# Last column block of a SwiGLU output product: token half 2 of its last four steps taken behind half 1, LayerNorm and output per half

## The chip, the cores and the metric

The kernel runs on one core of one Trainium2 chip. The core has a matrix engine (TensorE, "PE" in the profile, its weight loads "PEld"), a vector engine (VectorE, DVE), a scalar engine (ScalarE, ACT), GpSimd (POOL) and SyncE (SP), which issues most of the DMAs. The engines run at the same time, each takes its own instructions in order, and they wait for each other by semaphores. PE writes only to the small accumulator memory PSUM; the other engines read it from there. The metric is the device time of one execution in microseconds (us), the median of several runs.

## The reference

One decoder layer at batch 1, 256 tokens, width 2048, in float32. The change lies in the last lines, the second product of the SwiGLU (5632 to 2048) and the LayerNorm behind it:

```python
h = x * (1.0 + sc2) + sh2
gate, up = jnp.split(h @ w_ffn_in, 2, axis=-1)
y = (jax.nn.silu(gate) * up) @ w_ffn_out          # (256, 5632) @ (5632, 2048)
r = DEEPNORM_ALPHA * x + g2 * y
mu, var = r.mean(-1), jnp.square(r - r.mean(-1)).mean(-1)
x = (r - mu) * lax.rsqrt(var + LN_EPS) * ln2_g + ln2_b
```

The mean and the variance run over all 2048 columns of a token, so no token can be normalized before its last column is done.

## The kernel before

The 256 tokens are two halves of 128 (h = 0 and 1; "half 1" and "half 2" in the prediction), one token for each partition. A weight comes in tiles of 128x1024 that SP loads (`load_w`, L212, six buffers). ACT casts each to the reduced type float32r (`hi`, L221, four buffers), and DVE takes the rest (`lo`, L222, four buffers); PE multiplies with both, and so gets nearly full float32 precision. The activations are split the same way (`ach`, `acl`).

The output product is cut into four column blocks of 512 (`n` = 0 to 3). One block is 22 steps of two 128-row pieces of the weight each (`xs_unit`). A step has twelve products of 128x128 with 128x512: for each piece and each half, xh by hi (L356), xh by lo (L357) and xl by hi (L358). They add up in two PSUM tiles, `box[0]` and `box[1]`. Within a step the halves alternate; in the last step of a block half 1 comes ahead of half 2. `run(3)` writes the program so that about three splits are issued ahead of the step that PE is at. A scheduler then orders each engine's instructions by dependences and priorities.

At the end of a block `resid` (L1090) makes for each half t = ps*g2 (L1096), r = ALPHA*r + t (L1097) and bn_stats (L1098), and `fin` (L1315) multiplies r by the LayerNorm's gain (L1320). Behind the last block, `stats` (L1102) aggregates the mean and variance of both halves (L1106) and finds 1/sqrt(var + eps) with a Newton step (`rsqrt`, L365 to L372, its square root on ACT). `finish` (L1326) forms from -mean*rs, split in two, and ones a tile z of five columns; PE turns it (L1334) and ACT copies it to `zt` (L1336). With `rows`, five rows made of the gain and the bias, the product zt*rows (L1346, five rows deep) is the part of the output that isn't r*rs. DVE puts both together for every block of 128x512, r*rs + zt*rows (L1347), eight times, and SP writes the result out (L1351 for three blocks of both halves, 512 KB each, L1349 for the last block, 256 KB for each half).

The instructions in the names: `rt` is t, `st` the statistics, `mv` mean and variance, `le`, `lr`, `lrs` the steps of 1/sqrt, `mm` a PSUM tile of the pool with four such tiles, `tpm` the PSUM tile of the turned z, `raw` a loaded weight tile.

Of the kernel before, what the change touches and what calls it, by code (L numbers as in the profile page):

```python
# [93 lines left out]
def layer(ctx, tc, a, out):  # L94
# [995 lines left out]
    def resid(ps, c0, cn, gb, base, dst, st, n, then):  # L1090
        cc = slice(c0, c0 + cn)
        last = c0 + cn == D
        with tc.high_priority(offset=400 if last else 0):
            for h in range(2):
                t = acc("rt", [P, 512])[:, :cn]
                v_.tensor_tensor(t, ps[h], gb[:, cc], op=OP.mult)  # L1096
                v_.scalar_tensor_tensor(dst[:, h, cc], base[:, h, :], ALPHA, t, op0=OP.mult, op1=OP.add)  # L1097
                v_.bn_stats(st[:, h, n, :], dst[:, h, cc])  # L1098
# [190 lines left out]
    def fo_begin():  # L1289
        drain("main")  # L1290
        drain("ada")
        b0 = perm.tile([P, 2, D], F32, tag="s0", name="b0")
# [16 lines left out]
        cur["st"] = perm.tile([P, 2, 4, 6], F32, tag="stt", name="st2", bufs=2)

    do(fo_begin)
    for n, (c0, cn) in enumerate((512 * n, 512) for n in range(4)):
# [2 lines left out]
        def fin(ps, n=n, c0=c0, cn=cn):  # L1315
            cc = slice(c0, c0 + cn)
            r = cur["r"]
            resid(ps, c0, cn, cur["g2b"], r[:, :, cc], r, cur["st"], n, finish)
# [7 lines left out]
    def finish(mv, rs):  # L1326
        nm = perm.tile([P, 2, 1], F32, name="nm")
        z = cur["z"]
        v_.scalar_tensor_tensor(nm, mv[:, :, 0:1], -1.0, rs, op0=OP.mult, op1=OP.mult)
        v_.tensor_copy(z[:, :, 0:3:2], nm.to_broadcast([P, 2, 2]))  # L1330
        v_.tensor_tensor(z[:, :, 4:5], nm, z[:, :, 0:1].bitcast(F32), op=OP.subtract)
        tp = pt.tile([P, 512], F32, tag="tp", name="tpm")
        for h in range(2):
            t_.transpose(tp[0:5, h * P:(h + 1) * P], z[:, h, :].bitcast(F32), ident)  # L1334
        zt = cur["zt"] = cur["k3"].tile([5, 2, P], F32R, name="zt")
        s_.copy(zt, tp[0:5, :S].rearrange("p (h i) -> p h i", h=2))  # L1336
        cur["rs"] = rs
# [4 lines left out]
    for n in range(4):
        cc = slice(512 * n, 512 * n + 512)
        for h in range(2):
            ps = mm()
            t_.matmul(ps, cur["zt"][:, h], cur["rows"][:, cc], start=True, stop=True)  # L1346
            v_.scalar_tensor_tensor(r[:, h, cc], r[:, h, cc], rs[:, h], ps, op0=OP.mult, op1=OP.add)  # L1347
            if n == 3:
                dma.dma_start(out[0, h * P:(h + 1) * P, cc], r[:, h, cc])  # L1349
        if n < 3:  # L1350
            dma.dma_start(out[0, :, cc].rearrange("(h p) n -> p h n", p=P), r[:, :, cc])  # L1351
# [34 lines left out]
```

## Time and profile before

| | |
|---|---|
| time, median of 3 runs | 1697.94 us (1695.81 to 1700.74) |
| the profiled execution | 1696.81 us |
| its span, first to last instruction | 1694.9 us |
| mean granted clock of PE over the span | 0.994 of full speed |
| loads of the output product's weight | 88 of 512 KB, 4.1 us from issue to landing |
| ACT in the last column's steady state | a cast of 1.06 us every 2.72 us |

A row of the timeline has the start in us, the duration, the engine, the line of the kernel, the operation and its operands, shapes and count; in brackets the time that the engine was idle before it and what it waited for. A group's row has the operands, the count, the busy time in us and the mean of one in ns. Durations of PE overlap, since products are pipelined: the distance between starts says what one costs.

### The profile page before, as it was taken

To read this page: it belongs to the slowest core of one execution; us is meant where nothing else is said; L and a number is where in the kernel's file an instruction comes from. 1 tells how busy PE (TensorE), PEld (TensorE's weight loads), DVE (VectorE), ACT (ScalarE), POOL (GpSimd) and SP (SyncE) were. 2 spreads that over 40 slices of the span, in tenths; PEclk is the share of its full clock that TensorE was granted. 3 is DMA by queue.
4 is the path that set the end of the run, shared out by engine and by line. 5 is a ranking of instruction groups with operands and counts; after the bars stand their busy time and mean duration, and the time that the engine had idled before them with its cause. 6 is when DMAs were issued, how large, how long until landed. Compare 5 with 4: busy or idle time off the path is not lost.

```text
span 1694.9 us, 28166 instructions
## 1 busy us (share of the span) xinstructions
PE 1646.1 (97%) x11077; PEld 1478.7 (87%) x11077; DVE 1236.2 (73%) x1768; ACT 839.8 (50%) x1199; POOL 34.6 (2%) x60
## 2 busy tenths in 40 slices
PE   5899999999999999999999999999999999999997
PEld 4899999789989789889988898888888888888885
DVE  6899999687985678468998786666666666555454
ACT  3544445679653754464434454444444444333341
POOL 0000000001010000000000000000000000000000
PEclk9999999999999999999999999999999999999998
DMA  9999996566875578657999477777777777766651
GB/s 370 339 362 342 362 347 217 182 189 202 265 246 173 177 230 278 200 174 266 334 366 338 139 236 234 240 230 228 222 237 231 228 227 246 238 192 191 198 191 73
DMA packets 113751, 412.72 MB, mean 244 GB/s; under 512 B 13406, under 2 KB 14446, under 8 KB 108110
## 3 DMA queue, kind: packets, MB, share of 16 engines
q1 hardware_dynamic: 110178, 400.13, 70.2%
q0 software_dynamic: 3440, 10.80, 2.4%
q8 instruction: 87, 1.43, 0.3%
q14 instruction: 46, 0.37, 0.1%
HBM read 406.59 MB, written 4.28 MB: 242 GB/s over the span
## 4 chain that ended last, share of the span: by engine, by line
PE 62%; DVE 7%; DMA 4%; ACT 3%; issue 2%; POOL 0%; DVEq 0%; ACTq 0%; POOLq 0%
PE mm L315 17%; PE mm L319 9%; PE mm L356 7%; PE mm L358 7%; PE mm L357 7%; PE mm L308 4%; PE mm L309 4%; PE mm L310 3%; DVE lo L222 3%; DMA raw<-in_w_out 1%; DVE raw_a L241 1%; ACT hi L221 1%; DMA raw<-in_w_proj_gdn 1%; PE ps L756 1%; DMA UU<-ubd 0%
## 5 line engine op out<-in xcount | busy, mean ns | idle before, releaser
L222 DVE TENSOR_TENSOR lo<-raw,hi 128x1024 fp32r<-128x1024 f32 (+2 forms) x576 | 675.5, 1178 | 365.4 <-ACT hi L221 362.6
L221 ACT CAST hi<-raw 128x1024 fp32r<-128x1024 f32 (+2 forms) x576 | 583.6, 1017 | 721.5 <-PE mm L315 196.1
L308 PE MATMUL mm<-s,hi 128*128 128x256 f32 x1232 | 349.0, 284 | 16.1 <-ACT s L229 12.0
L310 PE MATMUL mm<-s,lo 128*128 128x256 f32 x1232 | 345.2, 281 | 8.1 <-DVE lo L222 7.9
L309 PE MATMUL mm<-s,hi 128*128 128x256 f32 x1232 | 345.1, 280 | 0.0
L315 PE MATMUL mm<-s,hi 128*128 128x512 f32 x1280 | 319.6, 392 | 0.0
L315 PEld LDWEIGHTS mm<-s,hi 128*128 128x128 f32 x1280 | 228.5, 188 | 39.5
L308 PEld LDWEIGHTS mm<-s,hi 128*128 128x128 f32 x1232 | 234.1, 190 | 21.3 <-ACT s L229 13.6
L310 PEld LDWEIGHTS mm<-s,lo 128*128 128x128 f32 x1232 | 234.1, 190 | 10.0 <-DVE lo L222 9.9
L309 PEld LDWEIGHTS mm<-s,hi 128*128 128x128 f32 x1232 | 234.4, 190 | 1.8 <-issue 1.4
L319 PEld LDWEIGHTS mm<-s,lo 128*128 128x128 f32 x1280 | 169.9, 188 | 13.6
L319 PE MATMUL mm<-s,lo 128*128 128x256 f32 x1280 | 171.9, 277 | 0.0
L357 PE MATMUL mm<-lo,ach 128*128 128x512 f32 x352 | 137.0, 389 | 0.0
L356 PE MATMUL mm<-hi,ach 128*128 128x512 f32 x352 | 137.0, 389 | 0.0
L358 PE MATMUL mm<-hi,acl 128*128 128x512 f32 x352 | 136.9, 389 | 0.0
L241 DVE CUSTOM_DVE_ANT_0 r<-r,cb,cols 128x2048 f32<-128x2048 f32 x40 | 93.5, 2348 | 9.2 <-ACT cb L137 9.2
L356 PE MATMUL mm<-hi,s 128*128 128x512 f32 x192 | 78.2, 407 | 0.0
L358 PEld LDWEIGHTS mm<-hi,acl 128*128 128x128 f32 x352 | 66.1, 188 | 13.8
L356 PEld LDWEIGHTS mm<-hi,ach 128*128 128x128 f32 x352 | 66.1, 188 | 13.7
L357 PEld LDWEIGHTS mm<-lo,ach 128*128 128x128 f32 x352 | 66.1, 188 | 13.5
L358 PE MATMUL mm<-hi,s 128*128 128x512 f32 x192 | 77.0, 401 | 0.0
L357 PE MATMUL mm<-lo,s 128*128 128x512 f32 x192 | 76.1, 396 | 0.0
(314 smaller groups left out, 2260.2 us busy)
## 6 DMA issues: line engine op xcount, KB each, us to landing
raw<-in_w_ffn_in SPq DMA_DIRECT2D x176, 512.0 KB, 4.3
raw<-in_w_in SPq DMA_DIRECT2D x160, 512.0 KB, 4.6
raw_a<-in_w_ada SPq DMA_DIRECT2D x112, 512.0 KB, 4.6
raw<-in_w_ffn_out SPq DMA_DIRECT2D x88, 512.0 KB, 4.1
r<-in_w_ada SPq DMA_DIRECT2D x40, 1024.0 KB, 8.1
raw<-in_w_in SPq DMA_DIRECT2D x48, 384.0 KB, 5.6
raw<-in_w_proj_gdn SPq DMA_DIRECT2D x32, 512.0 KB, 4.6
raw<-in_w_out SPq DMA_DIRECT2D x32, 512.0 KB, 6.3
```

Of the source, the lines that this page charges most:

```text
L221: s_.copy(hi, raw)
L222: low = v_.tensor_tensor(lo, raw, hi.bitcast(F32), op=OP.subtract)
L241: added = v_.tensor_tensor_reduce(out=raw, in0=raw, in1=cb[:, n * part:n * part + n], scale=1.0, scalar=cols[:, col:col + 1] if first else ...
L308: t_.matmul(o, hi[:, i, c], ah, start=(first and i == 0 and t == 0), stop=False)
L309: t_.matmul(o, hi[:, i, c], al, start=False, stop=False)
L310: t_.matmul(o, lo[:, i, c], ah, start=False, stop=(last and i == kn - 1 and t == 1))
L315: t_.matmul(box[t].rearrange("p (u i) -> p u i", u=2), hi[:, i, t * P:(t + 1) * P], both[k0 + i], start=(first and i == 0), stop=False)
L319: t_.matmul(box[t][:, :S], lo[:, i, t * P:(t + 1) * P], both[k0 + i][:, 0, :], start=False, stop=(last and i == kn - 1))
L356: t_.matmul(box[h], xh, hi[:, i, :], start=start, stop=False)
L357: t_.matmul(box[h], xh, lo[:, i, :], start=False, stop=False)
L358: t_.matmul(box[h], xl, hi[:, i, :], start=False, stop=stop)
L756: t_.matmul(ps[to, n, :], lhs(n), rhs(n), start=True, stop=True)
```

## The change

The last stage is written anew as `fo_unit`, `fo_column`, `scaled`, `fo_stats`, `fo_turn` and `fo_out`.

- In the blocks n = 0 to 2 the products stay in their order. Behind them come for both halves t, r and bn_stats, and then the scaling, at normal priority.
- In the block n = 3 the first 18 steps are as before. In the last four (`HOLD = 4`) only half 1's products are made at their place; the weights are kept, and half 2's products of the four steps follow in one piece.
- `end` puts half 1's statistics and scaling, which need only `box[0]`, ahead of half 2's held products, and half 1's turn of z and output behind them. Each half has its own z, zt and statistics. The square root is taken from the variance directly, with eps as its bias.
- Half 1's output is made by PE and ACT: PE multiplies a diagonal matrix of rs (`dg`, made by ACT from the identity) with r in plain float32, adds zt*rows in the same PSUM tile, and ACT copies the sum to r. Half 2's output is made by DVE as before. Two of half 1's PSUM tiles (`ps_o`) come from another pool.
- There are eight writes of 256 KB, one for each half and block.

```diff
+    def fo_column(ps, h, cc, n):
+        r = cur["r"]
+        t = acc("rt", [P, 512])
+        v_.tensor_tensor(t, ps, cur["g2b"][:, cc], op=OP.mult)
+        v_.scalar_tensor_tensor(r[:, h, cc], r[:, h, cc], ALPHA, t, op0=OP.mult, op1=OP.add)
+        v_.bn_stats(cur["st"][:, h, n, :], r[:, h, cc])
+
+    def scaled(h, cc):
+        r = cur["r"]
+        v_.tensor_tensor(r[:, h, cc], r[:, h, cc], cur["g"][:, cc], op=OP.mult)
+
+    def fo_stats(h):
+        own = cur["k3"].tile([P, 8], F32, name=f"fo{h}")
+        mv, e, q, rs, nm = [own[:, c:d] for c, d in ((0, 2), (2, 3), (3, 4), (4, 5), (5, 6))]
+        z = cur["z"][h]
+        v_.bn_aggr(mv, cur["st"][:, h])
+        s_.activation(q, mv[:, 1:2], AF.Sqrt, bias=epsc[:, 1:2])
+        v_.tensor_scalar(e, mv[:, 1:2], epsc[:, 1:2], -0.5, op0=OP.add, op1=OP.mult)
+        v_.reciprocal(q, q)
+        v_.tensor_tensor(rs, q, q, op=OP.mult)
+        v_.tensor_tensor(rs, rs, e, op=OP.mult)
+        v_.scalar_tensor_tensor(rs, rs, 1.5, q, op0=OP.add, op1=OP.mult)
+        v_.scalar_tensor_tensor(nm, mv[:, 0:1], -1.0, rs, op0=OP.mult, op1=OP.mult)
+        v_.tensor_copy(z[:, 0:3:2], nm.to_broadcast([P, 2]))
+        v_.tensor_tensor(z[:, 4:5], nm, z[:, 0:1].bitcast(F32), op=OP.subtract)
+        return rs
+
+    def fo_turn(h, rs):
+        tp = pt.tile([P, 512], F32, tag="tp", name="tpm")
+        t_.transpose(tp[0:5, :P], cur["z"][h].bitcast(F32), ident)
+        zt = cur["k3"].tile([5, P], F32R, name=f"zt{h}")
+        s_.copy(zt, tp[0:5, :P])
+        dg = k3_tile("sg")[:, 0, :P]
+        s_.activation(dg, ident, AF.Copy, scale=rs)
+        return zt, dg
+
+    def fo_out(h, n, rs, zt, dg, by_pe):
...
+        if by_pe:
+            t_.matmul(ps, dg, r[:, h, cc], start=True, stop=False)
+        t_.matmul(ps, zt, cur["rows"][:, cc], start=not by_pe, stop=True)
+        if by_pe:
+            s_.copy(r[:, h, cc], ps)
+        else:
+            v_.scalar_tensor_tensor(r[:, h, cc], r[:, h, cc], rs, ps, op0=OP.mult, op1=OP.add)
+        dma.dma_start(out[0, h * P:(h + 1) * P, cc], r[:, h, cc])
+
+    HOLD = 4
...
+        def end():
+            fo_column(box[0], 0, cc, n)
+            rs0 = fo_stats(0)
+            scaled(0, cc)
+            for x in held:
+                products(1, *x)
+            zt0, dg0 = fo_turn(0, rs0)
+            fo_column(box[1], 1, cc, n)
+            rs1 = fo_stats(1)
+            scaled(1, cc)
+            for m in range(3):
+                fo_out(0, m, rs0, zt0, dg0, m >= 0)
+            zt1, dg1 = fo_turn(1, rs1)
+            fo_out(0, 3, rs0, zt0, dg0, True)
+            for m in range(4):
+                fo_out(1, m, rs1, zt1, dg1, m >= 4)
...
+                else:
+                    products(0, k0, hi, lo)
+                    held.append((k0, hi, lo))
...
+                if n == 3:
+                    end()
+                    return
+                for h in range(2):
+                    fo_column(box[h], h, cc, n)
+                for h in range(2):
+                    scaled(h, cc)
...
-    r, rs = cur["r"], cur["rs"]
-    for n in range(4):
-        cc = slice(512 * n, 512 * n + 512)
-        for h in range(2):
-            ps = mm()
-            t_.matmul(ps, cur["zt"][:, h], cur["rows"][:, cc], start=True, stop=True)
-            v_.scalar_tensor_tensor(r[:, h, cc], r[:, h, cc], rs[:, h], ps, op0=OP.mult, op1=OP.add)
-            if n == 3:
-                dma.dma_start(out[0, h * P:(h + 1) * P, cc], r[:, h, cc])
-        if n < 3:
-            dma.dma_start(out[0, :, cc].rearrange("(h p) n -> p h n", p=P), r[:, :, cc])
```

In a row of the program order below, the line of the kernel comes first, then the operation, and what it writes and reads. Numbers behind a name tell buffers apart.

The first place is PE in the last step of the last block. Before, half 1 (`mm_16568`) and half 2 (`mm_16569`) take the same weights (`hi_16890`, `lo_16891`) one after the other, and the step before ended with half 2:

```order
L358 MATMUL mm_16569<-hi_16872,acl_10699 128x512
L356 MATMUL mm_16568<-hi_16890,ach_10698 128x512
L357 MATMUL mm_16568<-lo_16891,ach_10698 128x512
L358 MATMUL mm_16568<-hi_16890,acl_10699 128x512
L356 MATMUL mm_16568<-hi_16890,ach_10698 128x512
L357 MATMUL mm_16568<-lo_16891,ach_10698 128x512
L358 MATMUL mm_16568<-hi_16890,acl_10699 128x512
L356 MATMUL mm_16569<-hi_16890,ach_10698 128x512
```

Now half 1 (`mm_16570`) ends with the last step's weights (`hi_16892`), and half 2 (`mm_16571`) goes back to those of the fourth-last step (`hi_16838`):

```order
L1376 MATMUL mm_16570<-hi_16874,acl_10699 128x512
L1374 MATMUL mm_16570<-hi_16892,ach_10698 128x512
L1375 MATMUL mm_16570<-lo_16893,ach_10698 128x512
L1376 MATMUL mm_16570<-hi_16892,acl_10699 128x512
L1374 MATMUL mm_16570<-hi_16892,ach_10698 128x512
L1375 MATMUL mm_16570<-lo_16893,ach_10698 128x512
L1376 MATMUL mm_16570<-hi_16892,acl_10699 128x512
L1374 MATMUL mm_16571<-hi_16838,ach_10698 128x512
```

Half 2's 24 products of the last four steps have moved behind half 1's last.

The second place is what PE and ACT do behind the last weight product. PE now (`sg` is the diagonal, `mm` and `ps_o` the output tiles):

```order
L1376 MATMUL mm_16571<-hi_16892,acl_10699 128x512
L1341 MATMUL tpm_16960<-cst_77,z0_15340 5x128
L1356 MATMUL mm_16982<-r_9878,sg_16964 128x512
L1357 MATMUL mm_16982<-rows_15337,zt0_16962 128x512
L1356 MATMUL ps_o_16987<-r_9878,sg_16964 128x512
L1357 MATMUL ps_o_16987<-rows_15337,zt0_16962 128x512
L1356 MATMUL mm_16992<-r_9878,sg_16964 128x512
L1357 MATMUL mm_16992<-rows_15337,zt0_16962 128x512
L1356 MATMUL ps_o_17003<-r_9878,sg_16964 128x512
L1357 MATMUL ps_o_17003<-rows_15337,zt0_16962 128x512
L1341 MATMUL tpm_16997<-cst_77,z1_15341 5x128
L1357 MATMUL mm_17008<-rows_15337,zt1_16999 128x512
```

Three more products like the last row follow. On ACT there stood, behind the last cast, one square root and one copy of zt:

```order
L221 CAST hi_16872<-raw_16870 128x1024
L221 CAST hi_16890<-raw_16888 128x1024
L367 ACTIVATE lr_16955<-le_16954 128x2
L1336 CAST zt_16970<-tpm_16967 5x256
L1381 UNCONDITIONAL_BRANCH
```

Now there stand ten operations, those of half 2 (`fo1`, `zt1`) among half 1's copies:

```order
L221 CAST hi_16892<-raw_16890 128x1024
L1328 ACTIVATE fo0_16924<-fo0_16924,epsc_81 128x1
L1345 ACTIVATE sg_16964<-cst_77,fo0_16924 128x128
L1343 CAST zt0_16962<-tpm_16960 5x128
L1359 COPY r_9878<-mm_16982 128x512
L1359 COPY r_9878<-ps_o_16987 128x512
L1328 ACTIVATE fo1_16970<-fo1_16970,epsc_81 128x1
L1359 COPY r_9878<-mm_16992 128x512
L1345 ACTIVATE sg_17001<-cst_77,fo1_16970 128x128
L1359 COPY r_9878<-ps_o_17003 128x512
L1343 CAST zt1_16999<-tpm_16997 5x128
```

Half 2's square root has half 1's second copy ahead of it, and half 2's zt has the fourth; on PE, half 2's turn of z stands behind half 1's four outputs.

The third place is DVE between two blocks. Before, with the splits of the next block's weights (L222) in between:

```order
L1096 TENSOR_TENSOR rt<-mm,b_15320 128x512 x2
L1097 SCALAR_TENSOR_TENSOR r<-r,rt 128x512 x2
L1098 BN_STATS st_15342<-r 128x6
L222 TENSOR_TENSOR lo<-raw,hi 128x1024
L1320 TENSOR_TENSOR r<-r,b_15320 128x512
L1098 BN_STATS st_15342<-r 128x6
L222 TENSOR_TENSOR lo<-raw,hi 128x1024
L1320 TENSOR_TENSOR r<-r,b_15320 128x512
L222 TENSOR_TENSOR lo<-raw,hi 128x1024 x20
```

Now:

```order
L1315 TENSOR_TENSOR rt<-mm,b_15320 128x512 x2
L1316 SCALAR_TENSOR_TENSOR r<-r,rt 128x512 x2
L1317 BN_STATS st_15344<-r 128x6 x2
L1321 TENSOR_TENSOR r<-r,b_15320 128x512 x2
L222 TENSOR_TENSOR lo<-raw,hi 128x1024 x22
```

The next block's first split there has moved behind all eight operations.

More of the change, by code (lines that the diff above doesn't have):

```diff
@@ L1306, in fo_begin @@
         sdma.dma_start(rows[4:5], hld[0:1])
-        z = cur["z"] = k3.tile([P, 2, 5], F32R, name="z")
-        v_.memset(z.bitcast(F32), 1.0)
+        cur["z"] = [k3.tile([P, 5], F32R, name=f"z{h}") for h in range(2)]
+        for h in range(2):
+            v_.memset(cur["z"][h].bitcast(F32), 1.0)
         cur["st"] = perm.tile([P, 2, 4, 6], F32, tag="stt", name="st2", bufs=2)
+    def fo_column(ps, h, cc, n):
[4 more added lines that the diff above has]
+        v_.bn_stats(cur["st"][:, h, n, :], r[:, h, cc])
@@ new lines, in layer, with fo_unit, products, post @@
+    HOLD = 4
+    def fo_unit(n):
+        cc = slice(512 * n, 512 * n + 512)
+        box, held = [], []
+        def products(h, k0, hi, lo, some=range(2)):
+            for i in some:
+                k = k0 + i
+                xh, xl = [ops[k][:, h * P:(h + 1) * P] for ops in act_ops]
+                t_.matmul(box[h], xh, hi[:, i, :], start=k == 0, stop=False)
+                t_.matmul(box[h], xh, lo[:, i, :], start=False, stop=False)
+                t_.matmul(box[h], xl, hi[:, i, :], start=False, stop=k == FT - 1)
+        def end():
[14 more added lines that the diff above has]
+                fo_out(1, m, rs1, zt1, dg1, m >= 4)
+        for k0 in range(0, FT, 2):
+            def post(hi, lo, k0=k0):
+                if k0 == 0:
+                    box.extend([mm(), mm()])
+                if n < 3 or k0 < FT - 2 * HOLD:
+                    if k0 < FT - 2:
+                        for i in range(2):
+                            for h in range(2):
+                                products(h, k0, hi, lo, (i,))
+                    else:
+                        for h in range(2):
+                            products(h, k0, hi, lo)
+                else:
+                    products(0, k0, hi, lo)
+                    held.append((k0, hi, lo))
+                tick()
+                if k0 < FT - 2:
+                    return
+                if n == 3:
+                    end()
+                    return
+                for h in range(2):
+                    fo_column(box[h], h, cc, n)
+                for h in range(2):
+                    scaled(h, cc)
+            step(w_fo, k0, 2, 512 * n, 512, post)
@@ L1311, in layer @@
     do(fo_begin)
-    for n, (c0, cn) in enumerate((512 * n, 512) for n in range(4)):
+    for n in range(4):
         if n == 3:
             do(load_sqrt)
[L1315 to L1318, printed above, removed]
-            for h in range(2):
-                scaled = v_.tensor_tensor(r[:, h, cc], r[:, h, cc], cur["g"][:, cc], op=OP.mult)
-                if n == 3:
-                    tc.keep_in_program_order(scaled)
-        xs_unit(act_ops, w_fo, c0, FT, fin, cn)
@@ L1326, in finish @@
[L1326 to L1337, printed above, removed]
@@ L1339, in layer @@
-    run(3)
-    r, rs = cur["r"], cur["rs"]
-    for n in range(4):
-        cc = slice(512 * n, 512 * n + 512)
-        for h in range(2):
-            ps = mm()
[L1346 to L1349, printed above, removed]
-        if n < 3:
-            dma.dma_start(out[0, :, cc].rearrange("(h p) n -> p h n", p=P), r[:, :, cc])
+        fo_unit(n)
```

5 lines of the change are left out of this document (added).

## The prediction

> **What bounds the kernel now.** I read the page first, then a table of windows over the last column block, then the end of the timeline, row by row.
>
> ```profile
> span 1694.9 us, 28166 instructions
> PE 1646.1 (97%) x11077; PEld 1478.7 (87%) x11077; DVE 1236.2 (73%) x1768; ACT 839.8 (50%) x1199; POOL 34.6 (2%) x60
> ```
>
> PE is busy for 97% of the span, so a change can gain only where PE isn't. The windows say where that is (columns: window, length, busy time of PE, PEld, DVE, ACT, POOL, granted clock, DMA share, GB/s).
>
> ```profile
> 1618.90:1678.70 59.80, 59.80 (x265) 49.22 (x263) 28.68 (x29) 21.56 (x21) 0.00 (x0) 1.00 0.38 124
> 1678.70:1683.80 5.10, 0.04 (x1) 0.00 (x0) 4.52 (x17) 0.20 (x1) 0.00 (x0) 1.00 0.00 0
> 1683.80:1687.90 4.10, 3.62 (x9) 2.06 (x9) 3.55 (x6) 0.36 (x1) 0.00 (x0) 0.53 0.01 2
> 1687.90:1693.40 5.50, 1.20 (x2) 0.31 (x2) 2.99 (x5) 0.00 (x0) 0.00 (x0) 0.50 1.00 378
> 1693.40:1694.90 1.50, 0.00 (x0) 0.00 (x0) 0.00 (x0) 0.00 (x0) 0.00 (x0) 0.50 0.01 4
> ```
>
> The last column (first row) has no PE gap. Behind it lie 16.2 us: 5.1 of statistics on DVE with PE idle, 4.1 of turning z and starting the output, 5.5 in which the output is written at 378 GB/s, and 1.5 after the last byte. That tail is all that this change can shorten. Its rows (start, duration):
>
> ```profile
> 1676.99 0.39 PE L358 MATMUL mm<-hi,acl 128*128 128x512 f32 x1
> 1677.42 0.69 DVE L1096 TENSOR_TENSOR rt<-mm,b 128x512 f32<-128x512 f32 x1 [7.21 <-PE mm L358]
> 1678.14 0.69 DVE L1097 SCALAR_TENSOR_TENSOR r<-r,rt 128x512 f32<-128x512 f32 x1
> 1678.35 0.39 PE L358 MATMUL mm<-hi,acl 128*128 128x512 f32 x1
> ...
> 1680.75 0.64 DVE L1098 BATCH_NORM_STATS2 st<-r 128x6 f32<-128x512 f32 x1
> 1681.42 0.26 DVE L1106 BATCH_NORM_AGGREGATE mv<-st 128x2 f32<-128x24 f32 x1
> 1681.72 0.23 DVE L366 TENSOR_SCALAR le<-mv,epsc 128x2 f32<-128x2 f32 x1
> 1681.98 0.20 ACT L367 ACTIVATE lr<-le 128x2 f32<-128x2 f32 x1 [13.03 <-DVE le L366]
> 1682.22 0.17 DVE L368 RECIPROCAL lr<-lr 128x2 f32<-128x2 f32 x1 [0.27 <-ACT lr L367]
> ...
> 1683.62 0.16 DVE L1331 TENSOR_TENSOR z<-nm,z 128x2 fp32r<-128x2 f32 x1
> ...
> 1683.83 0.42 PE L1334 MATMUL tpm<-cst,z 128*5 128x128 f32 x2 [5.09 <-DVE z L1331]
> 1684.29 0.36 ACT L1336 CAST zt<-tpm 5x256 fp32r<-5x256 f32 x1 [2.10 <-PE tpm L1334]
> ...
> 1684.70 4.40 PE L1346 MATMUL mm<-rows,zt 5*128 5x512 f32 x8 [0.45 <-ACT zt L1336]
> 1685.53 5.36 DVE L1347 SCALAR_TENSOR_TENSOR r<-r,lrs,mm 128x512 f32<-128x512 f32 x8 [0.55 <-PE mm L1346]
> ...
> 1686.96 3.00 SPq L1351 DMA_DIRECT2D out<-r  x3
> ...
> 1690.26 1.22 SPq L1349 DMA_DIRECT2D out<-r  x2
> ```
>
> Six products separate the two L358 rows: (1678.35 - 1676.99) / 6 = 0.227 us each. DVE starts 0.43 after the start of the last product of a half. Dependent 512-wide DVE operations follow each other at 0.72 (1677.42 to 1678.14), small ones at 0.20 (seven steps, 1682.22 to 1683.62). The eight output operations end at 1690.89, 0.67 each.
>
> **Change, first part: half 2 held.** The last four steps hold 24 products per half. Half 1 now ends 24 x 0.227 = 5.44 us ahead of the end of half 2, which stays where it is: the last half-1 product starts at 1672.91. During its turn PE takes a step in 1.36 us instead of 2.72, so the weights must be there.
>
> ```profile
> 1667.70 0.39 PE L356 MATMUL mm<-hi,ach 128*128 128x512 f32 x1
> 1667.90 1.06 ACT L221 CAST hi<-raw 128x1024 fp32r<-128x1024 f32 x1 [1.66 <-PE mm L358]
> 1668.99 1.23 DVE L222 TENSOR_TENSOR lo<-raw,hi 128x1024 fp32r<-128x1024 f32 x1 [1.49 <-ACT hi L221]
> ```
>
> The first row starts the fourth-last step; the cast of the last step follows it at once, since it needs the buffers of the step before, which is not held. The split is complete at 1670.22; half 1 wants it at 1667.70 + 3 x 1.36 = 1671.78. Cover: 1.56 us, so cost nothing; without it PE waits microsecond for microsecond.
>
> **Second part: half 1's norm under half 2's products.** From rt at 1672.91 + 0.43 = 1673.34: two steps of 0.72, bn_stats to aggregate 0.67, aggregate 0.28, the 512-wide scaling now ahead of the small operations 0.6, eight small ones at 0.20: z ready near 1677.9. The products end being issued at 1678.58. All of it is hidden, with 0.7 us to spare.
>
> **Third part: half 1's output by PE and ACT.** Four blocks, each a plain-f32 product of diag(rs) with r, one of zt with rows, an ACT copy, a 256 KB write. The trace has no such pair, but has its pieces:
>
> ```profile
> L697 PE MATMUL g<-kq 128*128 128x512 f32 x16 | 8.2, 593 | 0.0
> 372.10 1.02 PE L697 MATMUL g<-kq 128*128 128x512 f32 x2
> L489 ACT COPY v<-mm 128x512 f32<-128x512 f32 x8 | 4.7, 585 | 7.8 <-PE mm L310 7.7
> L687 ACT ACTIVATE e<-gr,bcs 128x128 f32<-128x128 f32 x48 | 15.8, 395 | 3.5 <-DVE st L915 2.0 <-DVE ma L703 1.5
> ```
>
> A plain-f32 128x512 product runs as two passes of 0.593, together 1.02, so the second starts 0.43 after the first: 0.86 a product. Bounds: 0.23 (one pass, as above) and 1.19 (two passes that don't overlap); I take 0.86, the same operation and shape. With 0.23 for zt a block takes 1.09. Blocks run on PE from 1678.70 (z's turn is issued at 1678.58) and finish near 1679.98, 1681.07, 1682.16, 1683.24. ACT's copies (0.585) start behind each; the diagonal (0.395) fits ahead of 1678.58.
>
> **Fourth part: half 2's chain.** rt at 1678.78, where half 2's product always ended; aggregate over at 1681.17, scaling and L1329 until 1681.90. What waits is on ACT, in order: half 2's sqrt stands behind the second copy (over at 1681.67) and ends at 1681.90. No loss. Reciprocal to z: 1681.93 + 7 x 0.20 = 1683.3. On PE z's turn is queued behind the fourth block, issued by 1683.06. Turn 0.29: 1683.62. On ACT the fourth copy is ahead of zt: it ends at 1683.85, so zt is written from 1683.87 to about 1684.15. This wait costs 0.2. The first of four zt products starts at 1684.19, 0.51 sooner than 1684.70.
>
> ```profile
> L1346 PE MATMUL mm<-rows,zt 5*128 5x512 f32 x8 | 4.4, 705 | 0.5 <-ACT zt L1336 0.5
> L358 PE MATMUL mm<-hi,acl 128*128 128x512 f32 x352 | 136.9, 389 | 0.0
> ```
>
> Before, this product ran at a granted clock of 0.50 and DVE started 0.83 behind it; products of 512 columns at 1.00 let DVE start after 0.43. Between PE's blocks and these products only 1 us is idle, against 5.1 before, so I take 0.43: DVE's output starts at 1684.62, 0.91 sooner than 1685.53. At 0.83 it would be 0.40 later. [...]
>
> DVE then has four operations, not eight: 4 x 0.67 = 2.68 less, ending at 1687.3 instead of 1690.89: 3.59 us.
>
> **Fifth part: writes.** Data flowed from 1687.9, 0.9 behind the first issue, to 1693.4 at 378 GB/s, 2.5 behind DVE's last end. A 256 KB write alone needs 0.9 + 0.7 = 1.6. So 0.9 us of the tail is backlog. SP issues in order: half 1's four writes, which wait for ACT's copies, stand ahead of half 2's, but the last is issued at 1683.9, before half 2's first is ready (1685.3). Half 1's pieces are out by 1685.5, and half 2's come every 0.67, as fast as they are written. Bounds: 0 and 0.9; I take 0.8.
>
> **Elsewhere.** Columns 0 to 2 lose the interleaving:
>
> ```profile
> 1618.45 1.28 DVE L1096 TENSOR_TENSOR rt<-mm,b 128x512 f32<-128x512 f32 x2
> ...
> 1621.45 1.21 DVE L222 TENSOR_TENSOR lo<-raw,hi 128x1024 fp32r<-128x1024 f32 x1
> ```
>
> The first lo (fourth step of the next column) moves behind all eight operations, about 8 x 0.6 after 1618.45: 1623.3, done 1624.5. PE starts that step at 1618.9 + 3 x 2.72 = 1627.06. Hidden, by 2.6 us. The raw buffers come free at most 2 us later.
>
> **Sum.** 0.51 + 0.40 + 2.68 + 0.8 = 4.4 us. The profiled execution took 1696.81 (span 1694.9 and 1.9 around it), so 1692.4 for one like it; the median shown, 1697.94, lies 1.1 above, so I predict **1693.5**. The change is 0.26%; about 0.3% (5.1 us) is what a measurement of this kernel can tell from no change, and the three runs of before span 4.9 us.
>
> **Rivals.**
> - *The f32 products don't overlap* (1.19): a block takes 1.57 (0.593 x 2 + 0.389), the fourth finishes at 1685.1, its copy ahead of zt at 1685.7, the DVE output starts at 1686.5 and ends at 1689.2; gain 1.7 + 0.8 = 2.5, time 1695.4. For it: PE and ACT become the chain, with little slack. Against: the L697 pair overlaps.
> - *The held steps starve PE*: the last split is over 1.6 us late, and half 2 ends late by the rest. Three us late leave 1.4 of the gain: 1696.5. Against: that cast waits for PE alone, and DVE and ACT idle around it (the bracketed 1.66 and 1.49).
> - *More than forecast*: half 2's zt doesn't wait for the copy and the tail behind the last write shrinks too, over 5.1 us: 1692.5.
> - *Slower: the smaller writes don't overlap.*
>
> ```profile
> out<-r SPq DMA_DIRECT2D x2, 256.0 KB, 3.1
> ```
>
>   If half 2's four pieces landed one after another at 3.1, the last would land at 1685.3 + 12.4 = 1697.7, against 1690.9 + 3.1 = 1694.0: 3.7 slower, 1701.6. It loses from 2.2 us a piece on. Against: the window to 1693.40 shows 378 GB/s with two such pieces in it. [...]
>
> **How the numbers follow.** Forecast 0.62, products 0.18, starving 0.07, more 0.08, slower 0.05. The range: the bounds of the sum give gains of 1.7 (products apart, backlog unchanged) to 4.7 (no wait for the copy, whole backlog), 1693.2 to 1696.2; runs of before lie 2.1 below and 2.8 above their median, and part of that is added: 1691.3 to 1697.0. Faster by over 0.3% needs 0.7 us more than forecast: the case "more", 0.08, and 0.3 of the forecast by scatter, 0.19: 0.27. Slower by over 0.3%: 0.03. Within: 0.70.
>
> **What would show it.** Right: no PE gap from the fourth-last step to the fourth output block; rt of half 1 5.4 us before that of half 2; f32 pairs every 1.09; granted clock 1.00 until the last product; first DVE output 6.3 us after the last product starts (7.2 before); last bytes within 1.8 us of DVE's end. Wrong: PE waiting for ACT or DVE inside the held steps, zt of half 2 starting over 1.5 us later than 5.5 behind the last product, a granted clock of 0.50 in the output, or write rows far apart.

## The result, and the profile after

The changed kernel takes **1717.38 us** (median of 6 runs, 1715.13 to 1726.09) against 1699.09 for the kernel before (6 runs, 1695.81 to 1705.84): a ratio of **1.0111**, 95% interval 1.0091 to 1.0132. The forecast was 1693.5, a gain of 4.4 us. The kernel lost some 18 us instead.

First the page of the changed kernel: its span, and busy time, share and instructions of each engine.

```profile
span 1715.5 us, 28200 instructions
PE 1675.1 (98%) x11085; PEld 1498.2 (87%) x11085; DVE 1235.7 (72%) x1772; ACT 841.7 (49%) x1207; POOL 34.5 (2%) x60
```

PE has 8 instructions more and 29.0 us more of busy time, and is idle for 40.4 us of its span instead of 48.8; DVE, ACT and POOL stand where they stood. So PE was not kept waiting: the same products took longer. The view of one line (shortest, median and longest duration in ns, then first and last start in us) says where. Before:

```profile
L315 PE MATMUL mm<-s,hi x1280: 388/392/398, 999.5 to 1437.8; 128*128 128x512 f32 x183
L356 PE MATMUL mm<-hi,ach x352: 388/389/397, 1439.0 to 1677.9; 128*128 128x512 f32 x176
```

After (L356 has become L1374):

```profile
L315 PE MATMUL mm<-s,hi x1280: 392/394/399, 1011.1 to 1461.2; 128*128 128x512 f32 x183
L1374 PE MATMUL mm<-hi,ach x352: 387/389/397, 1462.3 to 1701.3; 128*128 128x512 f32 x176
```

L1374 is the last matmul, the only stage that the change rewrites. It lasts 239.0 us from first to last start, 238.9 before. But it begins at 1462.3 instead of 1439.0: **23.3 us are lost ahead of it**, in code that the diff doesn't touch, 11.6 of them ahead of L315 and 11.7 during it.

The windows show the pace inside two of those stages (columns as in the prediction; PE never idles in either). Before:

```profile
200.00:280.00 80.00, 80.00 (x708) 80.00 (x707) 77.96 (x100) 40.39 (x52) 2.57 (x4) 1.00 0.87 310
1040.00:1400.00 360.00, 360.00 (x2100) 316.56 (x2099) 233.82 (x284) 174.78 (x231) 0.00 (x0) 1.00 0.73 230
```

After:

```profile
200.00:280.00 80.00, 80.00 (x678) 80.00 (x677) 75.48 (x95) 38.94 (x50) 2.57 (x4) 1.00 0.86 303
1040.00:1400.00 360.00, 360.00 (x2044) 313.12 (x2043) 227.28 (x274) 168.47 (x224) 0.00 (x0) 1.00 0.71 225
```

PE is full, its clock is 1.00 in both, and yet 678 products pass where 708 did: 118.0 ns from one 256-column product to the next instead of 113.0. The second row has 2.7% fewer products. The durations in the view of a line hide this (a median of 392 ns became 394 for L315), since products overlap: the pace is read from counts in a window without gaps, not from the duration of one.

The end itself did what the change says. Rows of the changed kernel's timeline:

```profile
1696.71 0.69 DVE L1315 TENSOR_TENSOR rt<-mm,b 128x512 f32<-128x512 f32 x1 [3.13 <-PE mm L1376]
...
1700.91 0.16 DVE L1336 TENSOR_TENSOR z<-fo,z 128x1 fp32r<-128x1 f32 x1
...
1701.73 0.39 PE L1376 MATMUL mm<-hi,acl 128*128 128x512 f32 x1
...
1702.07 1.02 PE L1356 MATMUL mm<-r,sg 128*128 128x512 f32 x2
1702.15 0.69 DVE L1315 TENSOR_TENSOR rt<-mm,b 128x512 f32<-128x512 f32 x1 [1.08 <-PE mm L1376]
...
1703.02 0.49 PE L1357 MATMUL mm<-rows,zt 5*128 5x512 f32 x1
...
1703.44 1.12 PE L1356 MATMUL ps_o<-r,sg 128*128 128x512 f32 x2
...
1704.49 0.50 PE L1357 MATMUL ps_o<-rows,zt 5*128 5x512 f32 x1
...
1704.92 1.13 PE L1356 MATMUL mm<-r,sg 128*128 128x512 f32 x2
...
1707.02 0.16 DVE L1336 TENSOR_TENSOR z<-fo,z 128x1 fp32r<-128x1 f32 x1
...
1707.88 0.27 PE L1341 MATMUL tpm<-cst,z 128*5 128x128 f32 x1
...
1708.47 0.25 ACT L1343 CAST zt<-tpm 5x128 fp32r<-5x128 f32 x1
...
1708.77 1.23 PE L1357 MATMUL mm<-rows,zt 5*128 5x512 f32 x4 [0.62 <-ACT zt L1343]
...
1709.30 2.72 DVE L1361 SCALAR_TENSOR_TENSOR r<-r,fo,mm 128x512 f32<-128x512 f32 x4 [2.12 <-PE mm L1357]
```

From the last weight product (1701.73) to the end of the span are 13.8 us; before, from 1678.35 to 1694.9, 16.55. **The tail is 2.8 us shorter**, where 4.4 were forecast. 23.3 - 2.8 = 20.5 us is the difference of the two spans (20.6).

### The profile page after: what moved, and what is told of

It reads as the page before. It is cut to its first block, busy times and chain, and to the rows that moved or that the text cites. A ratio compares the mean times of both kernels' runs of the same rounds, so it can differ in the third digit from the quotient of the medians.

```text
span 1715.5 us, 28200 instructions
## 1 busy us (share of the span) xinstructions
PE 1675.1 (98%) x11085; PEld 1498.2 (87%) x11085; DVE 1235.7 (72%) x1772; ACT 841.7 (49%) x1207; POOL 34.5 (2%) x60
## 4 chain that ended last, share of the span: by engine, by line
PE 84%; DVE 5%; DMA 4%; ACT 4%; issue 2%; SPq 0%; POOL 0%; DVEq 0%; ACTq 0%; POOLq 0%
PE mm L315 17%; PE mm L308 9%; PE mm L310 9%; PE mm L309 9%; PE mm L319 9%; PE mm L1374 5%; PE mm L1375 5%; PE mm L1376 5%; PE mm L356 3%; PE mm L357 3%; PE mm L358 3%; DVE lo L222 2%; DMA raw<-in_w_out 1%; PE mm_kept L310 1%; PE mm_kept L308 1%
## 5 line engine op out<-in xcount | busy, mean ns | idle before, releaser
L222 DVE TENSOR_TENSOR lo<-raw,hi 128x1024 fp32r<-128x1024 f32 (+2 forms) x576 | 675.5, 1179 | 382.4 <-ACT hi L221 381.1
L308 PE MATMUL mm<-s,hi 128*128 128x256 f32 x1232 | 352.6, 287 | 15.1 <-ACT s L229 12.0
L310 PE MATMUL mm<-s,lo 128*128 128x256 f32 x1232 | 348.5, 284 | 6.5 <-DVE lo L222 6.5
L309 PE MATMUL mm<-s,hi 128*128 128x256 f32 x1232 | 349.1, 283 | 0.0
L315 PE MATMUL mm<-s,hi 128*128 128x512 f32 x1280 | 325.0, 395 | 0.0
L315 PEld LDWEIGHTS mm<-s,hi 128*128 128x128 f32 x1280 | 228.9, 188 | 44.6
L310 PEld LDWEIGHTS mm<-s,lo 128*128 128x128 f32 x1232 | 233.8, 190 | 8.1 <-DVE lo L222 8.0
L319 PEld LDWEIGHTS mm<-s,lo 128*128 128x128 f32 x1280 | 175.3, 188 | 14.1
L319 PE MATMUL mm<-s,lo 128*128 128x256 f32 x1280 | 178.2, 281 | 0.0
L1374 PE MATMUL mm<-hi,ach 128*128 128x512 f32 x352 | 136.9, 389 | 0.0
L356 PE MATMUL mm<-hi,s 128*128 128x512 f32 x192 | 78.6, 409 | 0.0
L1376 PEld LDWEIGHTS mm<-hi,acl 128*128 128x128 f32 x352 | 66.1, 188 | 13.8
L1374 PEld LDWEIGHTS mm<-hi,ach 128*128 128x128 f32 x352 | 66.1, 188 | 13.6
```

Of the source, the lines that this page charges most:

```text
L222: low = v_.tensor_tensor(lo, raw, hi.bitcast(F32), op=OP.subtract)
L308: t_.matmul(o, hi[:, i, c], ah, start=(first and i == 0 and t == 0), stop=False)
L309: t_.matmul(o, hi[:, i, c], al, start=False, stop=False)
L310: t_.matmul(o, lo[:, i, c], ah, start=False, stop=(last and i == kn - 1 and t == 1))
L315: t_.matmul(box[t].rearrange("p (u i) -> p u i", u=2), hi[:, i, t * P:(t + 1) * P], both[k0 + i], start=(first and i == 0), stop=False)
L319: t_.matmul(box[t][:, :S], lo[:, i, t * P:(t + 1) * P], both[k0 + i][:, 0, :], start=False, stop=(last and i == kn - 1))
```

## The experiments: why untouched code ran slower

**What changed without a line changing: addresses.** The old code had a tile `nm` of 8 bytes a partition in the pool `perm`, which lives through the whole kernel; the change drops it. In the two built programs every buffer that lies behind `perm`, the weight buffers raw, hi and lo among them, has moved down by 32 bytes, the room that `nm` took. Start addresses in SBUF, in bytes:

```
              before    after
hi (first)     90816    90784
lo (first)    107200   107168
ach           124608   124576
s0 / s1        31872 / 48512 in both (activations, in perm)
```

The theory: pace depends on these addresses. The rival: the pace comes from something else in the new code (its program order, its PSUM pools, its size). Two runs part them: the 32 bytes put back in the changed kernel, and taken out of the old one.

```diff
 e1_pad32 (changed kernel)
+        perm.tile([P, 8], F32, name="pad_perm")
 e2_before_low (kernel before)
-        nm = perm.tile([P, 2, 1], F32, name="nm")
+        nm = cur["k3"].tile([P, 2, 1], F32, name="nm")
```

> The changed kernel with one unused 32-byte tile in the pool perm, where the tile nm stood before the change; no instruction is added. Every buffer outside perm (weight tiles, activations of the first stages, ach, acl) lies again where it lay before the change; in the changed kernel they lie 32 bytes lower. Theory A (addresses: the 23 us lost ahead of the last column are PE's pace, 0.117 instead of 0.113 us for a 256-wide product, set by where its operands lie): the pace goes back to 0.113, the first L1374 starts near 1439 instead of 1462, and the time is 20.6 + 2.8 below the changed kernel's less what is scatter, 1693 to 1697, 0.15% below the kernel before. Theory B (the longer program or its waits slow PE, wherever the buffers lie): it stays at 1715 to 1718.

> The kernel before, with nothing changed but the tile nm, which is taken from the pool p3 instead of perm; so the weight tiles and all buffers behind perm lie 32 bytes lower, as in the changed kernel. Theory A: the pace of 256-wide products is 0.117 from the first stage on, and the time rises by some 23 us to about 1721. Theory B: it stays at 1698.

e1, the changed kernel with 32 unused bytes: 1692.76 us, ratio to before **0.9965** (0.9944 to 0.9986). Its windows:

```profile
200.00:280.00 80.00, 80.00 (x709) 80.00 (x708) 78.05 (x99) 40.34 (x54) 2.57 (x4) 1.00 0.86 308
1040.00:1400.00 360.00, 360.00 (x2099) 316.67 (x2098) 233.80 (x284) 174.26 (x230) 0.00 (x0) 1.00 0.73 230
```

e2, the old kernel without them: 1720.71 us, ratio **1.0101** (1.0070 to 1.0131):

```profile
200.00:280.00 80.00, 80.00 (x678) 80.00 (x678) 75.48 (x94) 38.14 (x49) 2.57 (x4) 1.00 0.86 301
1040.00:1400.00 360.00, 360.00 (x2045) 313.33 (x2044) 228.10 (x276) 168.12 (x223) 0.00 (x0) 1.00 0.70 224
```

The pace goes with the 32 bytes, in both directions, to the count. The loss is no part of the new last stage, and the new stage alone is a gain of 2.4 to 9.5 us by e1's interval (0.14 to 0.56% of 1700).

**Place or distance?** Is 32 bytes lower bad in itself, or the distance between what a product streams (s) and the weights that it loads? First other shifts: 64 bytes in `perm`, which puts all buffers 32 higher than before, and 32 bytes between the weight buffers and the rest (in `wp`, the pool of the weights).

```diff
 e3_pad64
+        perm.tile([P, 16], F32, name="pad_perm")
 e4_weights_low
+        wp.tile([P, 8], F32, name="pad_wp", bufs=1)
```

> The changed kernel with an unused tile of 64 bytes in perm: the buffers behind perm lie 32 bytes higher than before the change, 64 higher than in the changed kernel. Theory A in the form that a weight tile has to start at a multiple of 64 bytes: slow like the changed kernel, 1715 to 1718. In the form that only the place before was bad or good by its distance to the moving operand: another pace, between 0.113 and 0.118 and not the changed kernel's in every stage. Theory B: 1715 to 1718 with the changed kernel's pace in every stage.

> The changed kernel with an unused tile of 32 bytes at the end of the weight pool: raw, hi and lo stay 32 bytes lower than before the change, while everything behind that pool (ybA, mh, ach, acl and so on) is back at its place. Theory A with the weight tiles' own place as the cause in the stages whose activations lie in perm (s): there the pace stays 0.117, the first L1374 starts near 1462, 1713 to 1718 in all; the stages that read ybA, mh and ach with weights may change by 5 us in all. If instead the place of the other buffers is the cause: 1693 to 1697.

e3: 1717.12, ratio 1.0084 (1.0055 to 1.0113): 32 bytes up is as bad as down. e4, where raw, hi and lo alone lie lower: 1726.8, ratio 1.0139 (1.0114 to 1.0165), longer than the 1713 to 1718 expected. In the last matmul hi and lo are what PE streams, and ach is what it loads. There ach stayed in e4 while hi and lo moved, and this stage slowed as well, 245.8 us instead of 238.9 between first and last start:

```profile
L1375 PE MATMUL mm<-hi,ach x352: 392/396/397, 1465.0 to 1710.8; 128*128 128x512 f32 x176
```

That points to distance. Then runs that move no buffer: `aT` hands out s0 and s1 with 64 spare columns, and its second argument is the column (4 bytes) at which the data begin.

```diff
 e5_aligned (e1, distance 0 everywhere)
-    place["lo"] = 32
+    place["lo"] = 0
-    hTh, hTl = [aT(tag)...
+    hTh, hTl = [aT(tag, 16)...
-        halves = [aT(tag, 32)...
+        halves = [aT(tag, 16)...
 e11_after_s96 (changed kernel): aT(tag, 24) in both places
 e13_before_s32 (kernel before): aT(tag, 8), and aT(tag, 40) for the halves
 e14_after_s224 (changed kernel): aT(tag, 56), and aT(tag, 24) for the halves
```

> The kernel of e1 with the activations of the first projection and of the gate and up products put 64 bytes higher in the first case and 64 lower in the second, inside their own tiles, and lo at the start of its tile everywhere; no buffer moves and the program's order is the same. Then the start addresses of weight tile and activations differ by a multiple of 128 bytes in these stages, as they always do in the last product, which ran at 113.3 ns for 256 columns in five kernels; in e1 they differ by 64 and the stages ran at 114.1 to 114.7. Theory A in the form 'the distance modulo 128 bytes decides: 0 is always full pace, 32 and 96 are always slow, 64 is either': 113.3 everywhere in these stages, first L1375 some 8 us earlier than in e1 (1431 instead of 1439), time 1684 to 1688. Rival: 64 is as good as 0, only 32 is bad: the time of e1, 1691 to 1696.

> The changed kernel as it stands, its buffers 32 bytes lower, with the activations of the first projection put 96 bytes higher inside their own tiles and those of the gate and up products at the same 96 bytes (128 before); no buffer moves, the program's order is the same. e5 took away the theory that a distance of 0 is best for these stages. What fits all six layouts so far for products of 256 columns: start of activations less start of weight tile, modulo 128 bytes: 64 gives 113.3 to 114.5 ns (118 in some stages of some runs), 32 or 96 gives 118.4, 0 gives 119.9. Here it is 64 again, with the buffers at the changed kernel's bad place. If the distance decides: 114.3 in the s stages, first L1374 1440 to 1445 instead of 1462, time 1693 to 1699. If the place itself decides (weight tiles must not start at 32 bytes past a multiple of 64): 1715 to 1718.

> The kernel before with the same two groups of activations put 32 bytes (first projection) and 8 floats (gate and up products, 160 bytes for 128) further inside their tiles; no buffer moves, nothing else changes. Distance 96 modulo 128 in the s stages. If the distance decides: 118.4 ns, and the time rises by about 20 to 1715 to 1722, with the tail of the kernel before. If the place of the buffers decides: 1698.

> The changed kernel as it stands, buffers 32 bytes lower, with the first projection's activations 224 bytes higher inside their tiles (e11 had 96) and the gate and up products' at 96 as in e11. In e11 the gate and up stage was back at 114.3 (first pair of stages: the distance modulo 256 there is the kernel before's), but the first projection stayed at 117.8: its distance is 64 modulo 256, before it was 192. Taking the distance modulo 256, all nine layouts give for 256 columns 119.9 at 0, 117.8 at 64, 118.1 at 160, 113.3 to 114.5 (in some stages 118) at 192, 118.5 at 224. Here it is 192 again in both stages. If the distance modulo 256 decides: the first projection at 113.3 to 114.5, first L1374 at 1440 to 1443, time 1694 to 1698 (the stage that reads ya stays slow, some 1.5 us). If not, the first projection stays at 117 to 119 and the time at 1700 to 1704 as in e11.

s0 starts at 128 modulo 256 and hi at 192 before, so the projection's distance is 192 there; in gate/up the halves begin 32 columns (128 bytes) further on, and so does lo (`place["lo"]`, also in columns). Each kernel with the distance (start of s less start of the weights, modulo 256) in two stages, and the products that PE began there, from the windows as above. The first projection (200 to 280 us) has 256-column products only; the gate/up stage (1040 to 1400) takes s with hi in 512 columns and with lo in 256.

| kernel | projection | products | gate/up, hi and lo | products | median us | ratio (95%) |
|---|---|---|---|---|---|---|
| before | 192 | 708 | 64, 192 | 2100 | 1699.09 | 1 |
| after | 224 | 678 | 96, 224 | 2044 | 1717.38 | 1.0111 (1.0091, 1.0132) |
| e1 | 192 | 709 | 64, 192 | 2099 | 1692.76 | 0.9965 (0.9944, 0.9986) |
| e2 | 224 | 678 | 96, 224 | 2045 | 1720.71 | 1.0101 (1.0070, 1.0131) |
| e3 | 160 | 676 | 32, 160 | 2050 | 1717.12 | 1.0084 (1.0055, 1.0113) |
| e4 | 224 | 679 | 96, 224 | 2045 | 1726.80 | 1.0139 (1.0114, 1.0165) |
| e5 | 0 | 669 | 0, 0 | 2064 | 1716.16 | 1.0088 (1.0060, 1.0115) |
| e11 | 64 | 682 | 64, 192 | 2100 | 1702.61 | 1.0021 (1.0005, 1.0038) |
| e13 | 224 | 679 | 96, 224 | 2046 | 1722.42 | 1.0131 (1.0106, 1.0156) |
| e14 | 192 | 709 | 64, 192 | 2098 | 1696.31 | 0.9979 (0.9965, 0.9993) |

e13 and e14 decide it. e13 leaves every buffer of the old kernel where it is and streams s from 32 bytes further on: the old kernel becomes as slow as the changed one. e14 leaves every buffer of the changed kernel at its bad place and moves s to the old distance: the pace is back. So each of the two places of the weights has been fast with one place of s and slow with another; the pair decides, and neither place alone. The windows of e14:

```profile
200.00:280.00 80.00, 80.00 (x709) 80.00 (x708) 77.60 (x100) 39.79 (x51) 2.57 (x4) 1.00 0.88 313
1040.00:1400.00 360.00, 360.00 (x2098) 316.58 (x2097) 233.72 (x284) 173.83 (x229) 0.00 (x0) 1.00 0.72 230
```

Two guesses on the way were wrong. e5 was expected to be best, with distance 0, and has the slowest projection of all (80 us / 669 = 119.6 ns). e11 was built on a distance that counts modulo 128; it brought back the gate/up stage, where its distances are those of before, and left the projection, at 64 instead of 192, slow.

## The experiments: the tail

All four are e1 (the good addresses) with one more edit, so the end is all in which their programs differ. Tails are counted here from the start of the last product that reads ach, the second-last of all weight products, to the end of the span: 16.8 us before, 14.0 in the changed kernel and in e1.

**The hold** (`HOLD = 4` made `HOLD = 0`: both halves end in the old order).

> The kernel of e1 with HOLD = 0: no half-2 product is held, and half 1 ends 1.4 us ahead of half 2 as before; statistics per half, output by PE and ACT for half 1 as in the change. Both halves' statistics then share DVE behind the last product with PE idle. Theory: holding is what carries the gain; half 2's zt waits for half 1's blocks, which start some 5 us later: tail 17 to 20 us instead of 14.0, time 1696 to 1700, no better than the kernel before (tail 16.8). Rival: the output by two pairs of engines carries it: tail 14 to 15.5.

1704.90 us, ratio 1.0026 (1.0008 to 1.0044); tail 19.6. The tail is as expected, the time is longer than the 1696 to 1700 expected: the span ahead of the tail is 3.4 us longer than in e1, 1681.9 against 1678.5 (see the last section). Without the hold, the new end is worse than the old one. Two windows:

```profile
1683.00:1687.00 4.00, 0.00 (x0) 0.00 (x0) 4.00 (x15) 0.63 (x3) 0.00 (x0) 1.00 0.00 0
1687.00:1692.00 5.00, 4.59 (x8) 1.69 (x9) 1.23 (x11) 1.41 (x4) 0.00 (x0) 0.66 0.00 0
```

And of its timeline:

```profile
1687.41 1.67 PE L1357 MATMUL mm<-r,sg 128*128 128x512 f32 x2 [4.88 <-ACT sg L1346]
...
1689.08 1.92 PE L1357 MATMUL ps_o<-r,sg 128*128 128x512 f32 x2
...
1691.74 1.12 PE L1357 MATMUL mm<-r,sg 128*128 128x512 f32 x2
```

PE idles for 4.9 us, and the first pairs behind take 1.67 and 1.92 us instead of 1.02. The granted clock, 1.00 in the window before, is 0.66 in that one. In the kernel before, 5.1 us with PE idle were followed by 4.1 us at 0.53 (1683.80 to 1687.90). Without the hold the tail is 5.6 us longer, twice the whole gain of 2.8. That the hold is needed is shown by this; that it is enough is not, and the next run says that it isn't.

**Half 1's output by DVE** (`by_pe` False in both calls for half 1).

> The kernel of e1 with half 1's four output blocks by DVE too (four operations of 0.67 us, set among half 2's statistics) and no diagonal products or ACT copies. Theory: DVE waits some 2.9 us behind the last product in e1 (1.1 before half 2's rt, 0.6 at the root, up to 2.1 before the output), so only a part of the 2.7 is added: first output of half 2 0.3 to 1.0 us later than in e1, tail 14.3 to 15.0, time 1693 to 1697. Rival: PE and ACT are the slower pair here, since half 2's zt waits for them: tail 13.3 to 14.0.

Missed: 1696.67 us, ratio 0.9991 (0.9973 to 1.0009); tail 16.3, longer than expected. DVE has the products of zt early and fits half 1's four operations into half 2's statistics:

```profile
1677.66 0.69 DVE L1316 TENSOR_TENSOR rt<-mm,b 128x512 f32<-128x512 f32 x1 [1.09 <-PE mm L1377]
...
1678.61 0.75 DVE L1362 SCALAR_TENSOR_TENSOR r<-r,fo,mm 128x512 f32<-128x512 f32 x1 [0.26 <-PE mm L1358]
...
1684.31 0.16 DVE L1337 TENSOR_TENSOR z<-fo,z 128x1 fp32r<-128x1 f32 x1
...
1684.52 0.37 PE L1342 MATMUL tpm<-cst,z 128*5 128x128 f32 x1 [5.25 <-DVE z L1337]
...
1686.07 2.72 DVE L1362 SCALAR_TENSOR_TENSOR r<-r,fo,mm 128x512 f32<-128x512 f32 x4 [1.60 <-PE mm L1358]
```

Half 2's z comes 6.65 us after its rt, 4.87 in the changed kernel (1702.15 to 1707.02), and PE idles 5.25 us meanwhile. Moving the output to PE and ACT is thus worth about 2.3 us of tail beside the hold. With the hold alone the tail is 16.3, 0.5 shorter than before; with the output by PE and ACT alone it is 19.6, 2.8 longer. The two together give 2.8 less, so neither has a gain of its own that could be added up.

**Blocks in pairs** (for two blocks first both diagonal products, then both zt products).

> The kernel of e1 with half 1's output blocks made in pairs: two diagonal products, then two five-row products. In the changed kernel a block took PE 1.47 us where 1.09 was forecast. If the changes between the 128-row and the five-row products cost the extra 0.38 (theory: they don't overlap), a pair takes about 2.6 instead of 2.94, half 2's zt starts some 0.6 us earlier, and the tail behind the last weight product (14.0 us in e1) is 13.3 to 13.5. If the f32 products themselves are slower than 0.86, nothing is saved: 13.9 to 14.3. The time is 1692 to 1696 either way.

1694.64 us, ratio 0.9968 (0.9948 to 0.9987); tail 13.5, as expected. PE's rows:

```profile
1679.60 1.02 PE L1357 MATMUL mm<-r,sg 128*128 128x512 f32 x2
...
1680.46 1.02 PE L1357 MATMUL ps_o<-r,sg 128*128 128x512 f32 x2
...
1681.41 0.49 PE L1359 MATMUL mm<-rows,zt 5*128 5x512 f32 x1
...
1681.75 0.38 PE L1359 MATMUL ps_o<-rows,zt 5*128 5x512 f32 x1
...
1682.06 1.13 PE L1357 MATMUL mm<-r,sg 128*128 128x512 f32 x2
```

Diagonal product follows diagonal product after 0.86 us, as forecast, but a zt product starts 0.95 behind the last of them and the next diagonal product 0.31 behind the last zt product. Two blocks take 2.46, against 2.96 one by one. The half microsecond per two blocks lies in the change of kind: from a diagonal product (128 rows, plain float32) to a zt product (five rows, float32r) and back. Whether it is the rows or the type is not separated by any run.

**All together** (e8; half 2's zt copied by DVE; half 2's last block also by PE and ACT).

```diff
-        s_.copy(zt, tp[0:5, :P])
+        (v_.tensor_copy if h else s_.copy)(zt, tp[0:5, :P])
-                fo_out(1, m, rs1, zt1, dg1, m >= 4)
+                list(fo_out(1, m, rs1, zt1, dg1, m >= 3))
```

> The kernel of e8 (buffers at the place of before, pairs of blocks) with half 2's zt copied by DVE instead of ACT, and half 2's last block made by PE and ACT like half 1's. Theory: in e8 half 2's zt waits 0.55 us for ACT's fourth copy while DVE idles, and DVE's fourth output takes 0.66 while PE and ACT idle; the tail falls from 13.5 to 12.2 to 12.6, time 1690 to 1694, ratio to the kernel before 0.9950 to 0.9970. If the writes bound the end instead, the tail stays over 13.0.

1692.51 us, ratio **0.9955** (0.9936 to 0.9974); tail 13.0, a little longer than expected. DVE's output starts 6.55 us after the last product (1676.07; 7.57 in the changed kernel) and has three operations, but ACT's copy of the fourth block ends last, at 1685.16:

```profile
1681.75 0.28 DVE L1344 CAST zt<-tpm 5x128 fp32r<-5x128 f32 x1 [0.85 <-PE tpm L1342]
...
1682.62 2.07 DVE L1363 SCALAR_TENSOR_TENSOR r<-r,fo,mm 128x512 f32<-128x512 f32 x3 [0.59 <-PE mm L1359]
...
1684.57 0.59 ACT L1361 COPY r<-mm 128x512 f32<-128x512 f32 x1 [2.18 <-PE mm L1359]
```

It beats both kernels. Against e1 and e8 its interval doesn't part it; the traces put it 1.0 and 0.5 us ahead in the tail.

## Why the prediction was wrong

- **The step that failed is "Elsewhere"**, with the sentences it rests on: "a change can gain only where PE isn't" (busy) and "That tail is all that this change can shorten." They were used as if nothing outside the tail could get longer. Only DVE's order at the column boundaries was priced there; the pace of PE in all other stages was taken as given, and no rival touched it. The runs put 23.3 us in that place, five times the gain in question: products of 256 columns 118.0 ns apart instead of 113.0, and back when the distance was put back (e1, e14). What caused it stands in no line of the change that speaks of work: a tile of 8 bytes that is no longer allocated in a pool that lives all through.
- **Elsewhere as priced was right**: L1374 lasts 239.0 us, as before; the columns' boundaries cost nothing.
- **First part, the hold: right.** Half 1's rt stands at 1696.71, 5.44 us ahead of half 2's at 1702.15, to the digit, and PE has no gap.
- **Second part: right.** z is ready at 1701.07, and the last product starts at 1701.73: 0.66 to spare, 0.7 forecast.
- **Third part: mis-sized.** The pair took 1.02 as its row said, but a block 1.48 (1703.44 to 1704.92), not 1.09. I had let the zt product follow after 0.86 and the next block after 0.23; it was 1.05 and 0.43. The rival "the f32 products don't overlap" (1.57) had nearly the size, though for another reason: the two passes of a pair do overlap (1.02), and a pair follows a pair after 0.86 (e8); what costs is the change to and from the five-row product.
- **Fourth part: so the output started late.** Half 2's z was ready 4.87 us behind rt, but its turn stood behind the fourth block on PE until 1707.88, and zt behind the fourth copy on ACT until 1708.47. DVE's output began 7.57 us after the last product; 6.27 was forecast and 7.18 was before. That is 1.3 of the missing 1.6 us. The clock forecast held: while half 2's zt products started, from 1708.80 to 1709.60, the granted clock was 1.00, and DVE started 0.53 behind the first of them (0.43 taken; 0.83 before, at 0.50 from 1684.70 to 1687.90), and the four operations took 2.72 for 2.68.
- **Fifth part: a little less.** DVE ends at 1712.02, 3.5 us ahead of the span's end, 4.0 before: 0.5 for a forecast of 0.8. The backlog itself, 0.9, is gone: by the windows below, 30 GB/s over the last 2 us are some 0.16 us of writing at 385, so the last bytes come near 1713.7, 1.6 us behind DVE's end, as a write alone needs by the forecast. What is longer is the stretch behind the last byte, 1.8 us against the 1.5 of before; no run shows why. The last windows of the changed kernel:

```profile
1712.00:1713.50 1.50, 0.00 (x0) 0.00 (x0) 0.03 (x1) 0.00 (x0) 0.00 (x0) 0.50 1.02 385
1713.50:1715.50 2.00, 0.00 (x0) 0.00 (x0) 0.00 (x0) 0.00 (x0) 0.00 (x0) 0.50 0.08 30
```

  and, from the view of the DMA issues, pieces, size and median time to landing:

```profile
out<-r SPq DMA_DIRECT2D x8, 256.0 KB, 2.1
```

  The last small writes run at 385 GB/s, and the median of the eight lands in 2.1 us (3.1 before), so the rival "slower by writes" is out.
- With the addresses put right, e1 has 1692.76, where 1693.5 was predicted. That nearness is in part luck: its tail is 2.8 us shorter, not 4.4, its ten runs lie between 1691.00 and 1702.71, and e14, which has the same end and these two stages at the old distances, has 1696.31. And e1 is what the change was taken to be; it isn't the change that was made.

## What to carry to other kernels

Where an engine is busy for 97% of the span, a change can cost more through its pace in untouched stages than it gains in its own (23.3 us against 2.8 here); a tile added to or dropped from a pool that lives long can move everything allocated behind it (by 32 bytes here), so compare the addresses of old and new program along with their instructions. Test it with a pad of the same size before you judge the change, and read pace as products per window without gaps, not as the duration of one. Try it in both directions and in several runs, since one stage of one execution can show either pace (284 and 274 products in 32 us of the same projection in e9). On a chain of small products, try putting those of one kind together (e8: two blocks in 2.46 us instead of 2.96).

## What the runs showed of the hardware

- A stream of 256-column products runs at 113.0 ns a product (80 us / 708, the kernel before) or at 117.3 to 119.6 (682 in e11 to 669 in e5) at the same granted clock of 1.00, by the distance of the streamed operand's start from the weights' start in SBUF. Of the distances tried in the projection, modulo 256, only 192 ever ran at the fast pace; 0, 64, 160 and 224 were slow. For 512 columns the order is another: the gate/up stage, whose hi products are of that width, is fast at 64 (2100 products in the kernel before), while the last matmul slows in e4, from 238.9 to 245.8 us, when its streamed operand moves by 32. The six kernels with other distances in both stages took 0.8 to 1.4% longer than the kernel before (e3 1.0084, e4 1.0139).
- The distance 192 allows the fast pace and doesn't ensure it. Two stretches of the same projection, products of 256 columns that read the same s, in e9 (which has the addresses of e1) and then in e14:

```profile
104.00:136.00 32.00, 32.00 (x284) 32.00 (x283) 31.26 (x39) 13.48 (x17) 0.00 (x0) 1.00 0.96 373
200.00:232.00 32.00, 32.00 (x274) 32.00 (x273) 31.01 (x37) 14.47 (x19) 0.00 (x0) 1.00 0.93 328
```

```profile
104.00:136.00 32.00, 32.00 (x274) 32.00 (x273) 30.50 (x38) 13.11 (x16) 0.00 (x0) 1.00 0.96 369
200.00:232.00 32.00, 32.00 (x285) 32.00 (x284) 31.55 (x37) 15.44 (x20) 0.00 (x0) 1.00 0.97 352
```

  e9 turns from fast to slow and e14 from slow to fast. Between the stretches (144 to 168 us) PE stands still for over a microsecond in all, waiting for hi and lo. The other five traces at 192 have 284 or 285 products in both stretches, the seven traces at other distances 269 to 275. The same shows in the products that stream ybBh, a later stage of 256-column products. Their distance is 192, and the addresses are the same in e1 (first row) and in the kernel before (second row):

```profile
L308 PE MATMUL mm<-ybBh,hi x128: 275/276/277, 783.9 to 848.9; 128*128 128x256 f32 x128
L308 PE MATMUL mm<-ybBh,hi x128: 281/281/281, 784.7 to 852.2; 128*128 128x256 f32 x128
```

  They last 65.0 and 67.5 us from first to last start. So there is a second condition, which can change within one execution, and the slow projection of e11 at 64 might be that as well. It can't stand in for the distance: the six kernels with other distances in both stages (the changed one, e2 to e5, e13) have no run under 1710, and the kernel before has none over 1708.3. No run shows what in the chip ties pace to addresses.
- By the rows of the timeline, a five-row float32r product starts only 0.07 us ahead of the end of a plain-f32 pair of 128 rows (0.95 behind the start of a pair of 1.02, 1.05 behind one of 1.12, both in the changed kernel); a second pair starts 0.16 ahead of it (0.86 behind the start of a pair of 1.02, 0.97 behind one of 1.13, both in e8).
